# Gate/up weights: four of eight steps by seven products instead of three, two low parts by an accumulating transfer, and a pool mixer that takes its means first

## The chip, the cores and the metric

One core of one Trainium2 chip runs the whole program. The metric is the device time of one execution in microseconds; of several runs the median is given.

## The reference

A trunk of two layers on x of 256 tokens by 2048 channels, all in fp32. Each layer adds a token mixer and then a SwiGLU feed-forward net, both behind an RMS norm; at the end stands one more norm.

```python
for i in range(DEPTH):                      # 2
    hn = rmsnorm(h, norm_mix[i])
    if i % 2 == 0: mix = pool_mixer(hn, pool_w, pool_scale)   # means over 2, 4, 8, 16 tokens
    else:          mix = diff_attention(hn, ...)              # 8 heads, ALiBi, w_qkv, w_o
    h = h + mix
    h = h + swiglu(rmsnorm(h, norm_ffn[i]), w_gate[i], w_up[i], w_down[i])
return rmsnorm(h, final_norm)

swiglu(h, wg, wu, wd) = (silu(h @ wg) * (h @ wu)) @ wd        # 2048 -> 5632 -> 2048
```

The pool mixer takes, in each of four groups of 512 channels, the trailing mean less the token itself, and multiplies it with that group's 512 x 512 matrix.

## The kernel before

**Products.** Every weight element is used for 256 tokens. TensorE multiplies in fp32r, so an operand is split in a high part (a cast) and a low part (the operand less its high part), and a product is hi x hi + hi x lo + lo x hi: three matmuls. `split` does that for activations, `halves` (L114, L115) for weights: ACT casts whi, DVE subtracts to make wlo.

**Steps.** Weights come as raw tiles of 1 MB, 128 x 4 x 512, which `load` (L108) fetches on SP's queue into three buffers. A tile holds four blocks B12, B11, B22, B21 of a 2 x 2 product of blocks: two slices of the inner dimension by two column halves (for gate/up: 512 gate columns and 512 up columns); the left side's blocks are two slices by two tiles of 128 tokens. A *plain* step makes all eight block products, 8 x 3 = 24 matmuls of 128 x 512. A step *by seven products* makes seven, 21 matmuls, by the scheme of Strassen and Winograd: it needs sums of the weight's blocks (`sums`, tsum, L120 to L123, on DVE), their high and low parts (`sum_halves`, thi on ACT at L129, tlo on DVE at L130), and the activation's sums S1 to S4, made once in `pair` (L244 to L249). whi and wlo have three buffers each; tsum, thi and tlo have one each, in the pool of the feed-forward net.

**Groups.** `group` (its matmuls are L172) runs eight steps into eight PSUM banks, which the code names by the products: M1, M6, M7, P5, P3, P4, M2 and X are b0 to b7. A plain step adds to C11, C12, C21, C22, which are the banks M2, P3, P4 and X, that is b6, b4, b5 and b7. `combined` (L176 to L193) then makes the four results: ACT copies M1 (L182) and P5 (L186), DVE adds (L183 to L192), and each bank is free when its reader is done. Gate/up has eleven groups per layer, in chunks of 4, 4 and 3; behind each group ACT takes silu of the gate (L354) and DVE multiplies (L355), and TensorE transposes the result (L231) for the down product. Behind each chunk follow two down groups. SEVEN = (1, 4, 6) names the gate/up steps by seven: 5 x 24 + 3 x 21 = 183 matmuls per group. SEVEN_DOWN, SEVEN_QKV and SEVEN_O do it for the others.

**Order.** The program is written step by step, but a scheduler sets the order of each engine's instructions when the kernel is built; on the chip each engine then runs its list in order. Which matmuls stand next to each other at a group's end, and where a cast stands among ACT's copies, is thus decided there.

**Start and end.** At the start the pool mixer multiplies first and takes its means after: x comes transposed (x_t) for the products and as rows (x_n) for the residual; when the squares of the rows are summed (L212), z = product x row factor x scale (L310), and two or three small matmuls with a band matrix (L313, L315) take the means. Group 0 is multiplied in plain fp32 (L290), the others split (L303). At the end, behind the last row factor, eight DVE operations (L386) make x x factor x final gain, and four transfers carry it out.

Of the kernel before, what the change touches and what calls it, by code (L numbers as in the profile page):

```python
# [16 lines left out]
P = 128  # L17
# [9 lines left out]
WARM = 10  # L27
WINDOWS = (2, 4, 8, 16)
# [7 lines left out]
SEVEN = (1, 4, 6)  # L36
SEVEN_DOWN = (1, 4)
SEVEN_QKV = (1, 4)
SEVEN_O = ()

# [8 lines left out]
def trunk_kernel(ctx, tc, x_t, x_n, gains, scale_in, final_in, subln, lam_in, band, dist,  # L49
# [61 lines left out]
    def halves(raw, lo_block=0):  # L111
        hi = whl.tile([P, 4, 512], F32R, name="whi")
        lo = whl.tile([P, 4, 512], F32R, name="wlo")
        nc.scalar.copy(hi[:, lo_block:], raw[:, lo_block:])  # L114
        nc.vector.tensor_tensor(lo[:, lo_block:], raw[:, lo_block:], f32(hi[:, lo_block:]), ALU.subtract)  # L115
        return hi, lo
# [20 lines left out]
    def group(steps, pool):  # L137
# [15 lines left out]
        for (a, seven, src), step in zip(steps, plan):  # L153
            raw = load(src)
            t = sums(pool, raw) if seven else None
            w = [halves(raw, B11 if seven else 0)]
            if seven:
                w.append(sum_halves(pool, t))
            for b, parts in step:
# [3 lines left out]
                for at, which, block in parts:  # L163
                    hi, lo = w[which]
                    if seven:
                        ah, al = a[:, 0, at], a[:, 1, at]
                    else:
                        k, t = at
                        ah, al = (a[:, k, i, t * P:(t + 1) * P] for i in range(2))
# [26 lines left out]
    def rsqrt(ss, n, cols):  # L196


        v, s, t, r = (tmp.tile([P, 8], F32, name=f"rs_{x}") for x in "vstr")
# [9 lines left out]
    def square_sum(ss, t, j):  # L209

        sq = tmp.tile([P, 512], F32, name="sq", bufs=1)
        nc.scalar.activation(sq, x_tok[:, t, j * 512:(j + 1) * 512], AF.Square, accum_out=ss[:, t, j:j + 1])  # L212

    def row_scale(ss):
        tot = tmp.tile([P, 2], F32, name="ss_tot")
        nc.vector.tensor_reduce(tot, ss, AX.X, ALU.add)
        r = tmp.tile([P, 2], F32, name="r_tok", bufs=3)
# [40 lines left out]
    xp = operand()  # L258
    xq = operand(SEVEN)
    ss = tmp.tile([P, 2, 4], F32, name="ss")  # L260
    with tc.tile_pool(name="start", bufs=1, reuse_waits="tile") as st:
        band_sb = st.tile([P, 4, 3, P], F32, name="band_sb")
        scale_sb = st.tile([P, D], F32, name="scale_sb")
        xf = st.tile([P, NK, S], F32, name="xf")
        nc.scalar.dma_start(out=gain_sb, in_=gains)

        warm = tmp.tile([P, 8], F32, name="warm", bufs=1)
# [5 lines left out]
        def load_x(k0, k1):  # L273
            nc.sync.dma_start(out=xf[:, k0:k1, :], in_=x_t[:, k0 * S:k1 * S].rearrange("p (k s) -> p k s", s=S))


        w0 = st.tile([P, 4, 512], F32, name="w0")
        load_x(0, 1)
        nc.sync.dma_start(out=w0[:, 0:2], in_=pool_w[0][:, 0:2])
        load_x(1, 4)  # L280
        nc.sync.dma_start(out=w0[:, 2:4], in_=pool_w[0][:, 2:4])
        load_x(4, 8)
        x0 = st.tile([P, 4, S], F32, name="x0")
        zp = [None] * 4

        zp[0] = [acc() for _ in range(2)]
        for k in range(4):
            nc.vector.tensor_scalar(x0[:, k, :], xf[:, k], gain_sb[:, 0, k:k + 1], None, ALU.mult)
            for t in range(2):
                nc.tensor.matmul(zp[0][t], x0[:, k, t * P:(t + 1) * P], w0[:, k], start=(k == 0), stop=(k == 3))  # L290

        def group_product(g):
            zp[g] = [acc() for _ in range(2)]
            hi, lo = halves(load(pool_w[g]))
            if g < 3:
                load_x(4 * g + 4, 4 * g + 8)
            for k in range(4 * g, 4 * g + 4):
                a = tile_of(xp, k)
                split(a, xf[:, k], gain_sb[:, 0, k:k + 1])
                for t in range(2):  # L300
                    ah, al = (a[:, i, t * P:(t + 1) * P] for i in range(2))
                    for i, (u, w) in enumerate(((ah, hi), (ah, lo), (al, hi))):
                        nc.tensor.matmul(zp[g][t], u, w[:, k % 4], start=(k % 4 == 0 and i == 0),  # L303
                                         stop=(k % 4 == 3 and i == 2))

        def group_mean(g):
            cols = slice(g * 512, (g + 1) * 512)
            z = st.tile([P, 2, 512], F32, name="z", bufs=2)
            for t in range(2):
                nc.vector.scalar_tensor_tensor(z[:, t], zp[g][t], r[:, t:t + 1], scale_sb[:, cols], ALU.mult, ALU.mult)  # L310
            for t in range(2):
                ps = aux()
                nc.tensor.matmul(ps, band_sb[:, g, t], z[:, t], start=True, stop=(t == 0))  # L313
                if t:
                    nc.tensor.matmul(ps, band_sb[:, g, 2], z[:, 0], start=False, stop=True)  # L315
                nc.vector.tensor_tensor(x_tok[:, t, cols], ps, x_tok[:, t, cols], ALU.add)
                square_sum(ss, t, g)
            transposed(xq, g, 2, SEVEN)

        group_product(1)  # L320
        nc.sync.dma_start(out=x_tok, in_=x_n)
        ss_in = tmp.tile([P, 2, 4], F32, name="ss")
        for t in range(2):
            for j in range(4):
                square_sum(ss_in, t, j)
        r = row_scale(ss_in)
        nc.sync.dma_start(out=band_sb, in_=band)
        nc.sync.dma_start(out=scale_sb, in_=scale_in)
        nc.sync.dma_start(out=dist_sb, in_=dist)
        group_product(2)  # L330
        group_mean(0)
        group_product(3)
        group_mean(1)
        group_mean(2)
# [261 lines left out]
```

## Time and profile before

| | |
|---|---|
| three runs | 1902.51, 1901.35, 1902.2 us; median 1902.2 |
| the profiled execution | 1902.04 us by itself, its span 1900.1 us |
| mean granted TensorE clock | 0.989 |
| instructions | 20741 |
| HBM read, written | 355.39 MB, 2.10 MB |
| DMA | 189 GB/s over the span, 52% of 16 engines |

The profile is one execution on the chip. Times are microseconds from the start of the span; PE is TensorE, DVE VectorE, ACT ScalarE, POOL GpSimd and SP SyncE; L172 is line 172 of the kernel. A line of the timeline gives start, duration, engine, operation with output and inputs, and in brackets the idle time ahead of it with what ended it. The duration of a matmul is that of its way through the array; how often one starts is read from the distance of starts. A row of the chain of waits is a piece of the path that ended last.

### The profile page before, as it was taken

What the parts mean: (1) busy time and instruction counts of PE and PEld (TensorE: products, weight loads), DVE (VectorE), ACT (ScalarE), POOL (GpSimd) and SP (SyncE); (2) the same over time, 40 slices, a digit from 0 to 9 for tenths busy, and PEclk for the clock granted to TensorE, in tenths of its full rate; (3) what the DMA queues carried; (4) which work ended last, traced back from release to release, by engine and by line L of the source; (5) the groups of instructions that cost most, each with busy time, mean ns of one, the idle gap of its engine ahead of it and who ended that gap; (6) DMA issues with size and microseconds to landing.
All of it is one profiled execution on the core that took longest, in us unless ns stands there. A gap on an engine that the chain in (4) does not pass through costs nothing.

```text
span 1900.1 us, 20741 instructions
## 1 busy us (share of the span) xinstructions
PE 1852.9 (98%) x8204; PEld 1506.3 (79%) x8204; DVE 1571.1 (83%) x1591; ACT 1013.6 (53%) x983; POOL 0.7 (0%) x6
## 2 busy tenths in 40 slices
PE   8999999999999999999999999999999999999997
PEld 5678888888888887777777778888888888888885
DVE  5888987888878998987786645998878999878887
ACT  5555544555544556655555544655544555445554
POOL 0000000000000000000000000000000000000000
PEclk8999999999999999999999999999999999999998
DMA  8355555555555554544444444555555555565552
GB/s 308 141 191 199 200 191 201 187 205 207 196 189 211 185 199 176 187 168 155 166 147 153 177 140 170 199 198 181 206 212 201 198 200 199 194 225 186 201 200 101
DMA packets 51152, 358.82 MB, mean 189 GB/s; under 512 B 6000, under 2 KB 6256, under 8 KB 8432
## 3 DMA queue, kind: packets, MB, share of 16 engines
q1 hardware_dynamic: 50080, 355.36, 52.0%
q10 hardware_dynamic: 976, 2.15, 0.3%
q8 instruction: 64, 1.05, 0.2%
q14 instruction: 32, 0.26, 0.0%
HBM read 355.39 MB, written 2.10 MB: 188 GB/s over the span
## 4 chain that ended last, share of the span: by engine, by line
PE 92%; DVE 4%; ACT 2%; issue 1%; DMA 1%; SPq 0%; DVEq 0%; ACTq 0%
PE b L172 88%; PE b L231 2%; DVE wlo L115 1%; DMA x_tok<-x_n 1%; PE b L303 1%; ACT sq L212 1%; ACT whi L114 1%; PE b L313 0%; PE b L438 0%; DVE tsum L120 0%; DVE y L386 0%; DVE x_tok L373 0%; DVE s_sb L440 0%; DVE oT L224 0%; DVE xp L224 0%
## 5 line engine op out<-in xcount | busy, mean ns | idle before, releaser
L172 PE MATMUL b<-whi,xp 128*128 128x512 f32 x2804 | 905.8, 393 | 8.8 <-DVE c L189 3.0
L114 ACT CAST whi<-raw 128x2048 fp32r<-128x2048 f32 (+1 forms) x331 | 587.2, 1780 | 601.9 <-PE b L172 465.5
L115 DVE TENSOR_TENSOR wlo<-raw,whi 128x2048 fp32r<-128x2048 f32 (+1 forms) x331 | 701.0, 2123 | 219.2 <-ACT whi L114 217.7
L172 PEld LDWEIGHTS b<-whi,xp 128*128 128x128 f32 x2804 | 526.9, 189 | 126.9 <-ACT e L244 5.7
L172 PE MATMUL b<-wlo,xp 128*128 128x512 f32 x1402 | 549.9, 392 | 0.6 <-DVE wlo L115 0.5
L172 PE MATMUL b<-whi,h 128*128 128x512 f32 x1168 | 370.3, 390 | 1.1 <-ACT e L244 1.1
L172 PEld LDWEIGHTS b<-wlo,xp 128*128 128x128 f32 x1402 | 264.7, 189 | 55.6 <-DVE wlo L115 1.4
L172 PEld LDWEIGHTS b<-whi,h 128*128 128x128 f32 x1168 | 218.7, 188 | 47.0 <-ACT e L244 2.1
L130 DVE TENSOR_TENSOR tlo<-tsum,thi 128x2048 fp32r<-128x2048 f32 x102 | 233.1, 2286 | 19.8 <-ACT thi L129 19.3
L172 PE MATMUL b<-wlo,h 128*128 128x512 f32 x584 | 227.5, 390 | 0.1
L172 PE MATMUL b<-thi,xp 128*128 128x512 f32 x624 | 220.0, 394 | 0.0
L129 ACT CAST thi<-tsum 128x2048 fp32r<-128x2048 f32 x102 | 194.8, 1910 | 30.7 <-DVE tsum L123 30.7
L172 PEld LDWEIGHTS b<-thi,xp 128*128 128x128 f32 x624 | 116.5, 188 | 24.0 <-ACT thi L129 0.8
L120 DVE TENSOR_TENSOR tsum<-raw 128x1024 f32<-128x1024 f32 x102 | 124.5, 1220 | 7.6 <-DMA raw<-w_down 4.8
L172 PEld LDWEIGHTS b<-wlo,h 128*128 128x128 f32 x584 | 109.6, 188 | 23.5 <-DVE wlo L115 0.6
L172 PE MATMUL b<-tlo,xp 128*128 128x512 f32 x312 | 121.8, 390 | 0.0
L172 PE MATMUL b<-whi,oT 128*128 128x512 f32 x256 | 82.7, 402 | 2.2 <-DVE oT L224 2.2
L122 DVE TENSOR_TENSOR tsum<-tsum,raw 128x512 f32<-128x512 f32 x102 | 70.4, 690 | 2.4
L123 DVE TENSOR_TENSOR tsum<-tsum,raw 128x512 f32<-128x512 f32 x102 | 70.1, 687 | 1.9
L172 PEld LDWEIGHTS b<-tlo,xp 128*128 128x128 f32 x312 | 58.6, 188 | 12.1 <-DVE tlo L130 0.2
L172 PE MATMUL b<-thi,h 128*128 128x512 f32 x192 | 67.6, 393 | 0.3 <-ACT thi L129 0.3
L172 PEld LDWEIGHTS b<-whi,oT 128*128 128x128 f32 x256 | 49.2, 193 | 12.9 <-issue 2.6
(121 smaller groups left out, 1137.0 us busy)
## 6 DMA issues: line engine op xcount, KB each, us to landing
raw<-w_gu SPq DMA_DIRECT2D x176, 1024.0 KB, 4.8
raw<-w_down SPq DMA_DIRECT2D x88, 1024.0 KB, 4.8
raw<-w_qk SPq DMA_DIRECT2D x32, 1024.0 KB, 4.9
raw<-w_v SPq DMA_DIRECT2D x16, 1024.0 KB, 4.8
raw<-w_o SPq DMA_DIRECT2D x16, 1024.0 KB, 4.8
raw<-pool_w SPq DMA_DIRECT2D x3, 1024.0 KB, 16.9
x_tok<-x_n SPq DMA_DIRECT2D x1, 2048.0 KB, 13.7
xf<-x_t SPq DMA_DIRECT2D x3, 512.0 KB, 10.0
```

Source lines behind the costliest of these rows:

```text
L114: nc.scalar.copy(hi[:, lo_block:], raw[:, lo_block:])
L115: nc.vector.tensor_tensor(lo[:, lo_block:], raw[:, lo_block:], f32(hi[:, lo_block:]), ALU.subtract)
L120: nc.vector.tensor_tensor(t[:, T1:T3 + 1], raw[:, B11:B22 + 1], raw[:, B12:B12 + 1].broadcast_to([P, 2, 512]), ALU.add)
L122: nc.vector.tensor_tensor(t[:, T2], t[:, T1], raw[:, B22], ALU.add)
L123: nc.vector.tensor_tensor(t[:, T4], t[:, T2], raw[:, B21], ALU.add)
L129: nc.scalar.copy(hi, t)
L130: nc.vector.tensor_tensor(lo, t, f32(hi), ALU.subtract)
L172: nc.tensor.matmul(ps[b], x, y[:, block], start=first, stop=(left[b] == 0))
L212: nc.scalar.activation(sq, x_tok[:, t, j * 512:(j + 1) * 512], AF.Square, accum_out=ss[:, t, j:j + 1])
L231: nc.tensor.transpose(ps[:, i, 1 - t if seven else t], src(i, t), ident)
L303: nc.tensor.matmul(zp[g][t], u, w[:, k % 4], start=(k % 4 == 0 and i == 0), stop=(k % 4 == 3 and i == 2))
```

## The change

**Steps.** SEVEN becomes (1, 3, 5, 7): four of the eight gate/up steps go by seven, 4 x 24 + 4 x 21 = 180 matmuls, and the last step is now one of them. In the first group of each layer only step 7 does (7 x 24 + 21 = 189). SEVEN_QKV becomes (1, 5).

**Low parts.** In steps 0 and 4 of gate/up (ADDED) the low part is not subtracted by DVE. ACT writes -w, rounded to fp32r, into a tile with a tag of its own ("added", one buffer) and casts whi as before; then a transfer issued by GpSimd adds w, fetched once more from HBM, onto -w in place. That is 2 x 22 = 44 transfers of 1 MB.

**Start.** x_t is gone. x_n comes first in four pieces, the squares and the row factor follow, and the band matrix is scaled by the row factor; each group then takes its means by matmuls (x as rows times band) and multiplies them with the weights, two groups in plain fp32 and two split.

**End.** x x final gain is made beside the last down group; behind the row factor only a scaling is left, four on ACT and four on DVE. Some small buffers are shared to make room.

```diff
-SEVEN = (1, 4, 6)
+SEVEN = (1, 3, 5, 7)
-SEVEN_QKV = (1, 4)
+SEVEN_QKV = (1, 5)
+ADDED = (0, 4)
...
-    def halves(raw, lo_block=0):
+    def halves(raw, lo_block=0, added=None):
         hi = whl.tile([P, 4, 512], F32R, name="whi")
+        if added:
+            pool, src = added
+            lo = pool.tile([P, 4, 512], F32R, name="wlo", tag="added")
+            nc.scalar.activation(lo, raw, AF.Copy, scale=-1.0)
+            nc.scalar.copy(hi, raw)
+            nc.gpsimd.dma_start(out=lo, in_=src, accum_op=ALU.add)
+            return hi, lo
...
-            w = [halves(raw, B11 if seven else 0)]
+            w = [halves(raw, B11 if seven else 0, (pool, src) if i_step in added else None)]
...
+        for t in range(2):
+            for i in range(2):
+                cols = slice(i * 1024, (i + 1) * 1024)
+                nc.sync.dma_start(out=x_tok[:, t, cols], in_=x_n[:, t, cols])
...
+            r = rsqrt(tot[:, 0:1], D, 1)
+            part = band_sb[:, :, 0:2] if t == 0 else band_sb[:, :, 2:3]
+            nc.vector.tensor_scalar(part, part, r, None, ALU.mult)
...
-                    cs = combined(group([(xq[p], p in SEVEN, w_gu[layer][g, p]) for p in range(NP)], hp), hp)
+                    by_seven = SEVEN[-1:] if g == 0 else SEVEN
+                    cs = combined(group([(xq[p], p in by_seven, w_gu[layer][g, p]) for p in range(NP)], hp, ADDED), hp)
...
-                        nc.vector.scalar_tensor_tensor(y[:, t], x_tok[:, t, cols], r[:, t:t + 1],
-                                                       final_sb[j // 2][:, cols.start % 1024:cols.start % 1024 + 512],
-                                                       ALU.mult, ALU.mult)
+                        if t:
+                            nc.vector.tensor_scalar(ys[j][:, t], ys[j][:, t], r[:, t:t + 1], None, ALU.mult)
+                        else:
+                            nc.scalar.activation(ys[j][:, t], ys[j][:, t], AF.Copy, scale=r[:, t:t + 1])
```

The new file is longer: L172 (the matmuls) becomes L189, L114 (whi) L127 and L123 for the added steps, where L122 writes -w; L115 (wlo) becomes L128 and the transfer is L124; L120, L122, L123 (tsum) become L133, L135, L136; L129 and L130 (thi, tlo) L142 and L143; the copies of `combined` L199 and L203, its DVE operations L200 to L209; the transposes L248; silu and the product behind it L379 and L380; the work at the end L408, L419, L421.

What the scheduler makes of it is shown at two boundaries of layer 0. A name's number is a running one: a tile with a higher number is of a later step or group. First TensorE at the boundary of gate/up groups 6 and 7, before: b7_3147 and b4_3133 belong to step 0 of group 7 (weights 3122, 3123), and thi_3164, tlo_3165 and whi_3160 to its step 1.

```order
L172 MATMUL b7_3147<-wlo_3123,xp_91 128x512
L231 MATMUL b5_3099<-ident_75,c12_3081 128x128
L231 MATMUL b6_3113<-ident_75,c12_3081 128x128
L172 MATMUL b7_3147<-whi_3122,xp_91 128x512 x2
L172 MATMUL b7_3147<-wlo_3123,xp_91 128x512
L172 MATMUL b7_3147<-whi_3122,xp_91 128x512
L172 MATMUL b1_3175<-thi_3164,xp_92 128x512
L172 MATMUL b2_3179<-thi_3164,xp_92 128x512
L172 MATMUL b3_3183<-thi_3164,xp_92 128x512
L172 MATMUL b4_3133<-whi_3160,xp_92 128x512
L172 MATMUL b4_3133<-wlo_3161,xp_92 128x512
L172 MATMUL b1_3175<-tlo_3165,xp_92 128x512
```

The same place after; thi_3099 and tlo_3100 are those of step 7 of group 6, whi_3205, wlo_3206, thi_3209 and tlo_3210 those of step 1 of group 7.

```order
L189 MATMUL b4_2868<-whi_3095,xp_90 128x512
L189 MATMUL b5_2875<-thi_3099,xp_90 128x512
L189 MATMUL b5_2875<-tlo_3100,xp_90 128x512
L189 MATMUL b5_2875<-thi_3099,xp_90 128x512
L189 MATMUL b0_3213<-whi_3205,xp_84 128x512
L189 MATMUL b0_3213<-wlo_3206,xp_84 128x512
L189 MATMUL b0_3213<-whi_3205,xp_84 128x512
L189 MATMUL b1_3220<-thi_3209,xp_84 128x512
L189 MATMUL b2_3224<-thi_3209,xp_84 128x512
L189 MATMUL b3_3228<-thi_3209,xp_84 128x512
L189 MATMUL b1_3220<-tlo_3210,xp_84 128x512
L189 MATMUL b1_3220<-thi_3209,xp_84 128x512
```

Before, the last step's thi lay 39 matmuls ahead of the first use of the next (thi_3025 belongs to step 6), and 44 ahead of the first use of tlo. Now 3 matmuls lie between the last use of thi_3099 and the first of thi_3209, and 6 before the first of tlo_3210; step 0's matmuls follow behind. At the other boundaries of two gate/up groups the new order has 14 and 21 (1 to 2, 4 to 5), 15 and 31 (5 to 6), 30 and 31 (0 to 1, 2 to 3), and 3 and 6 again (8 to 9, 9 to 10); into the down groups it has 3 and 24 behind group 3, 13 and 38 behind group 7, and 13 and 50 behind group 10. Layer 1 has the same.

ScalarE at this place before: c11_3080 and c22_3083 are the copies of M1 and P5, whi_3195 is the cast of step 2 of the next group.

```order
L129 CAST thi_3025<-tsum_3017 128x2048
L114 CAST whi_3122<-raw_3120 128x2048
L182 COPY c11_3080<-b0_2865 128x512
L186 COPY c22_3083<-b3_2880 128x512
L114 CAST whi_3160<-raw_3154 128x1536
L129 CAST thi_3164<-tsum_3156 128x2048
L354 ACTIVATE c11_3080<-c11_3080,r_tok_450 128x512
L114 CAST whi_3195<-raw_3193 128x2048
L354 ACTIVATE c21_3082<-c21_3082,r_tok_450 128x512
```

And after, where whi_3240 is the cast of step 2; it takes the buffer of step 7's whi, whose last reader is the first row of TensorE's rows above (P3, bank b4).

```order
L142 CAST thi_3099<-tsum_3091 128x2048
L127 CAST whi_3205<-raw_3199 128x1536
L199 COPY c11_3124<-b0_2903 128x512
L203 COPY c22_3127<-b3_2918 128x512
L127 CAST whi_3240<-raw_3238 128x2048
L379 ACTIVATE c11_3124<-c11_3124,r_tok_460 128x512
L142 CAST thi_3209<-tsum_3201 128x2048
L379 ACTIVATE c21_3126<-c21_3126,r_tok_460 128x512
```

Before, thi of the next group (thi_3164) stood ahead of the first silu and of the cast of step 2. Now the cast of step 2 and the first silu stand ahead of thi_3209.

VectorE at the boundary of groups 5 and 6, before; c12, c21, c11 and c22 are the results that `combined` makes of group 5's banks.

```order
L115 TENSOR_TENSOR wlo_2820<-raw_2817,whi_2819 128x2048
L183 TENSOR_TENSOR c12_2784<-b1_2575,c11_2783 128x512
L123 TENSOR_TENSOR tsum_2853<-tsum_2853,raw_2851 128x512
L185 TENSOR_TENSOR c21_2785<-b2_2579,c12_2784 128x512
L184 TENSOR_TENSOR c11_2783<-b6_2526,c11_2783 128x512
L187 TENSOR_TENSOR c12_2784<-c22_2786,c12_2784 128x512
L115 TENSOR_TENSOR wlo_2858<-raw_2851,whi_2857 128x1536
L188 TENSOR_TENSOR c22_2786<-c22_2786,c21_2785 128x512
L189 TENSOR_TENSOR c12_2784<-b4_2533,c12_2784 128x512
```

And after:

```order
L128 TENSOR_TENSOR wlo_2896<-raw_2889,whi_2895 128x1536
L200 TENSOR_TENSOR c12_2821<-b1_2606,c11_2820 128x512
L133 TENSOR_TENSOR tsum_2891<-raw_2889 128x1024
L201 TENSOR_TENSOR c11_2820<-b6_2557,c11_2820 128x512
L202 TENSOR_TENSOR c21_2822<-b2_2610,c12_2821 128x512
L135 TENSOR_TENSOR tsum_2891<-tsum_2891,raw_2889 128x512
L204 TENSOR_TENSOR c12_2821<-c22_2823,c12_2821 128x512
L136 TENSOR_TENSOR tsum_2891<-tsum_2891,raw_2889 128x512
L205 TENSOR_TENSOR c22_2823<-c22_2823,c21_2822 128x512
L206 TENSOR_TENSOR c12_2821<-b4_2564,c12_2821 128x512
```

Bank b4, which the next group's step 0 takes, is freed by L189 before and by L206 after. Before, one low part and a sum of the next group stood among the operations ahead of it; now it is the whole tsum, in three operations, behind the low part of step 1. TensorE takes up b4 at this boundary right behind the three matmuls of M1 of step 1; the same holds at the boundaries 2 to 3 and 0 to 1.

More of the change, by code (lines that the diff above doesn't have):

```diff
@@ L135, in trunk_kernel, with group @@
     C11, C12, C21, C22 = M2, P3, P4, X
-    def group(steps, pool):
+    def group(steps, pool, added=()):
         plan = []
@@ L284, in trunk_kernel @@
-        zp = [None] * 4
[L286 to L290, printed above, removed]
+        band_sb = st.tile([P, 4, 3, P], F32, name="band_sb")
+        for t in range(2):
+            for i in range(2):
+                cols = slice(i * 1024, (i + 1) * 1024)
+                nc.sync.dma_start(out=x_tok[:, t, cols], in_=x_n[:, t, cols])
@@ L292, in group_product @@
+        scale_sb = st.tile([P, D], F32, name="scale_sb")
+        nc.scalar.dma_start(out=scale_sb, in_=scale_in)
+        nc.scalar.dma_start(out=dist_sb, in_=dist)
+        zp = [None] * 4
         def group_product(g):
             zp[g] = [acc() for _ in range(2)]
[L294 to L304, printed above, removed]
@@ L307, in group_mean, with residual @@
+        def residual(g):
             cols = slice(g * 512, (g + 1) * 512)
-            z = st.tile([P, 2, 512], F32, name="z", bufs=2)
             for t in range(2):
[L310 to L316, printed above, removed]
+                y = st.tile([P, 512], F32, name="y", bufs=2)
+                nc.vector.tensor_tensor(y, zp[g][t], scale_sb[:, cols], ALU.mult)
+                nc.vector.tensor_tensor(x_tok[:, t, cols], y, x_tok[:, t, cols], ALU.add)
@@ L317, in group_mean @@
                 square_sum(ss, t, g)
             transposed(xq, g, 2, SEVEN)
+        group_product(0)
         group_product(1)
[L321 to L329, printed above, removed]
+        residual(0)
```

106 lines of the change are left out of this document (70 added, 36 removed).

## The prediction

> **What bounds the kernel now.** I read the page first: the table of engines and the chain of work that ended last.
>
> ```profile
> PE 1852.9 (98%) x8204; PEld 1506.3 (79%) x8204; DVE 1571.1 (83%) x1591; ACT 1013.6 (53%) x983; POOL 0.7 (0%) x6
> PE 92%; DVE 4%; ACT 2%; issue 1%; DMA 1%; SPq 0%; DVEq 0%; ACTq 0%
> ```
>
> TensorE is the bound: 98% busy, 92% of the chain. So I asked next where it waits. In the two stretches that hold ten of eleven gate/up groups and the down groups of each layer (107 to 703 and 1231 to 1883 us) it never does: in the table of stretches, whose columns are length, busy time of PE, PEld, DVE, ACT and POOL, granted clock, DMA share and GB/s, busy time equals length. The third row is one gate/up group.
>
> ```profile
> 107.00:703.00 596.00, 596.00 (x2660) 491.91 (x2659) 519.28 (x448) 311.13 (x230) 0.00 (x0) 1.00 0.55 198
> 1231.00:1883.00 652.00, 652.00 (x2913) 537.99 (x2912) 569.04 (x493) 340.29 (x260) 0.00 (x0) 1.00 0.54 194
> 197.60:240.00 42.40, 42.40 (x192) 34.81 (x191) 38.81 (x36) 23.60 (x20) 0.00 (x0) 1.00 0.55 199
> ```
>
> A group takes 42.4 us; DVE works 38.8 of it, ACT 23.6. DVE is the second bound, with 3.6 us to spare, but sets nothing today. The price of one product is the distance of two matmul starts in the timeline:
>
> ```profile
> 86.27 0.39 PE L172 MATMUL b<-thi,xp 128*128 128x512 f32 x1
> 86.50 0.39 PE L172 MATMUL b<-tlo,xp 128*128 128x512 f32 x1
> ```
>
> that is 0.23; over many rows 0.2277 us (183 of them and the transposes make the 42.4).
>
> **Fewer products.** Twenty groups go from 183 to 180 matmuls, the two first groups from 183 to 189: 20 x 3 - 2 x 6 = 48 fewer, 48 x 0.2277 = **-10.9 us**. That is the whole gain on the bounding engine in the layers, and it comes only if TensorE goes on without waiting.
>
> **What changes at a group's end.** This is the step I rest on. The trace of before has one place, in the first group, where a released buffer is followed by the same casts; here are PE, ACT and DVE there (start, duration, engine):
>
> ```profile
> 90.58 0.62 PE L172 MATMUL b<-whi,xp 128*128 128x512 f32 x2
> 94.83 1.20 PE L172 MATMUL b<-thi,xp 128*128 128x512 f32 x4
> 97.69 0.40 PE L172 MATMUL b<-tlo,xp 128*128 128x512 f32 x1
> 105.15 0.79 PE L172 MATMUL b<-whi,xp 128*128 128x512 f32 x1 [2.98 <-DVE c L189]
> ```
>
> ```profile
> 91.05 1.91 ACT L114 CAST whi<-raw 128x2048 fp32r<-128x2048 f32 x1 [4.59 <-PE b L172]
> 92.87 1.91 ACT L129 CAST thi<-tsum 128x2048 fp32r<-128x2048 f32 x1
> 104.79 0.72 ACT L354 ACTIVATE c<-c,r_tok 128x512 f32<-128x512 f32 x1
> ```
>
> ```profile
> 93.00 2.29 DVE L115 TENSOR_TENSOR wlo<-raw,whi 128x2048 fp32r<-128x2048 f32 x1 [2.00 <-ACT whi L114]
> 95.21 2.29 DVE L130 TENSOR_TENSOR tlo<-tsum,thi 128x2048 fp32r<-128x2048 f32 x1
> 97.41 1.75 DVE L115 TENSOR_TENSOR wlo<-raw,whi 128x1536 fp32r<-128x1536 f32 x1
> 99.08 0.68 DVE L183 TENSOR_TENSOR c<-b,c 128x512 f32<-128x512 f32 x1
> 99.68 1.22 DVE L120 TENSOR_TENSOR tsum<-raw 128x1024 f32<-128x1024 f32 x1
> 100.81 0.68 DVE L184 TENSOR_TENSOR c<-b,c 128x512 f32<-128x512 f32 x1
> ```
>
> TensorE's last use of a buffer (start 90.58) released ACT 0.47 later; whi and thi in a row put the first matmul of thi at 94.83, 4.25 after that start, and wlo and tlo put the first of tlo at 97.69, 7.11 after. From start to start on a full queue a cast costs 1.82, a low part 2.21 (1536 columns: 1.67), a combining operation 0.60, the first sum 1.13.
>
> At a boundary of the old order the last step is plain: thi was last used 39 to 42 matmuls (9 us) before the next thi is wanted, and the products M1, M6, M7 and P5 end 24 matmuls (5.5 us) before the group does, so all but the last sums are done under them. In the new order the last step is by seven, and both covers go. thi, tlo and tsum have one buffer each, so thi of the next group's step 1 is cast after the last matmul of this group. Five kinds of boundary follow from the order; t = 0 is the start of the last matmul of P3, and after three more matmuls the group is over.
>
> *Kind A* (groups 6 to 7, 8 to 9, 9 to 10 of a layer; the rows are in the section on the change). PE wants thi 7 matmuls on, at 1.59. ACT: whi of step 2 waits for P3, 0.47 to 2.29; silu, with 0.6 (its row has 0.72 by itself), to 2.9; thi to 4.8; PE goes on at 4.87, **3.28 late**. DVE: wlo of step 2 from 2.4 to 4.64, a combining operation to 5.24, tlo to 7.53; PE has 3 thi matmuls to do first and would want tlo at 5.55; it gets it at 7.72, **2.17 late**. Sum 5.45 us.
>
> *Kind B* (2 to 3, 5 to 6, and 0 to 1). PE wants bank b4 at 1.59 for step 0. It is freed by L206, ahead of which stand eight DVE operations, begun at about -0.4, when wlo of step 1 is done: 7 x 0.60 + 1.13, and 0.60 of its own, put its end at 5.5; stall 4.1, then 1.2 for the two last results: 5.3 (5.65 for 0 to 1, where the activation table is loaded too). *Kind C* (1 to 2, 4 to 5): three short waits, 0.56 + 0.47 + 0.99 = 2.0. *Kind D*: the chain into the first down group after group 3, 3.8. *Kind E*: into the others, 1.0 each.
>
> Per layer 3 x 5.45 + 2 x 5.3 + 5.65 + 2 x 2.0 + 3.8 + 2 x 1.0 = 42.4; two layers: **+85 us**. Below it lies 0, if the order ran as it does now; half of it, 42, if only the first wait of each place remained. I take the whole, because both chains are the quoted ones, and the waits cannot move: the order on each engine is fixed.
>
> **The clock after a stall.** The stall of 2.98 us before 105.15 was followed by a stretch at half the clock:
>
> ```profile
> 102.17:105.15 2.98, 0.01 (x1) 0.00 (x0) 2.98 (x6) 2.95 (x3) 0.00 (x0) 0.99 0.07 22
> 105.15:108.40 3.25, 3.25 (x8) 2.57 (x9) 2.87 (x4) 2.78 (x3) 0.00 (x0) 0.50 0.87 302
> ```
>
> 8 matmuls in 3.25 us where 14.3 would fit: 1.4 us lost. The new order has 14 stalls of 3.28 or more, so 0 to 20; part of it falls into waits that come anyway. I take a third, **+7**.
>
> **The accumulating transfers.** 44 low parts leave DVE. It loses 2 x 2.21 us per group and gains one step by seven (about 6.4 - 2.2), so stays near 38; ACT gains 44 casts of 1.8. The nearest rows for the transfer itself are the plain load of the same 1 MB and the one of 2 MB beside other loads:
>
> ```profile
> raw<-w_gu SPq DMA_DIRECT2D x176, 1024.0 KB, 4.8
> x_tok<-x_n SPq DMA_DIRECT2D x1, 2048.0 KB, 13.7
> ```
>
> It reads two streams, is issued by POOL and shares the engines with SP's loads, so I take 8 us, between 4.8 and 13.7. What it may take without a wait is set by its one buffer ("added"): the matmuls from the last use of one to the first of the next, less the cast of -w. For step 0 that is 12.4 to 16.5 us: no wait. For step 4 it is 35 x 0.2277 - 1.9 = 6.0 in group 2, 7.0 in 5 and 7, 6.9 in 9, 9.5 in 10, 13 elsewhere. At 8: 2.0 + 1.0 + 1.0 + 1.1 = 5.1 per layer, **+10**; at 4.8 nothing; at 12 about +47. Layer 1's first group has 2.8 us of lead: **+5**.
>
> The Trainium skill, DMA: Bandwidth & Descriptors, "Anatomy of one DMA", fits a GpSimd transfer by 2.0 us plus its bytes over 436,000 per us: an estimate of 4.4 us for this one, by which the two terms would be 0 and the sum 15 lower. No trace here shows such a transfer.
>
> **Start.** First the chain, then the timeline, then L172 alone in the stretch:
>
> ```profile
> 3.76 1.08 SPq L274
> 4.89 13.74 DMA x_tok<-x_n
> 23.94 0.73 ACT sq L212 x2
> 26.39 0.76 DVE z L310
> 64.82 26.17 PE b L172 x114
> ```
>
> ```profile
> 6.18 7.11 PE L290 MATMUL b<-w,x 128*128 128x512 f32 x16 [0.49 <-DMA w<-pool_w]
> ```
>
> ```profile
> 6.18:64.82 58.64, 7.44 (x25) 4.21 (x25) 0.91 0.63 249
> ```
>
> At 64.82 the first group had 25 of its matmuls done, so the start proper ends at 64.82 - 5.7 = 59.1. In the new kernel TensorE begins when x_tok is there (3.8 + 2 x 4.8 = 13.4), its last half row squared (1.5) and the factor known (26.39 less 24.67, 1.7): about 17. Then it has 16 plain products of 0.87 (7.11 for 8), 16 means of 384 columns (0.65), 48 split products and 32 transposes of about 0.12: 39 us. It ends at 56: -3. The first group then lacks the 2.98 us stall and its slow stretch: -4.4. But its first accumulated part is wanted as soon as it is begun: 8 us and the hand-over, +9. Together **+2**; with x_tok at its old 13.7 us, +6; with a short transfer, -7.
>
> **Tail.** From the timeline of before:
>
> ```profile
> 1891.03 5.39 DVE L386 SCALAR_TENSOR_TENSOR y<-x_tok,r_tok,final_sb 128x512 f32<-128x512 f32 x8
> 1892.47 3.04 SPq L389 DMA_DIRECT2D out_t<-y  x2
> ```
>
> Eight operations of 0.67 on DVE become four on DVE and four on ACT: up to -2.7; the 2 MB that leave set part of the end, so **-1.3**. The products with the final gain lie ahead, beside the last down group.
>
> **Sum.** 1902.0 (the profiled run's own time; its span is 1900.1, the median of the runs 1902.2) - 10.9 + 85 + 7 + 10 + 5 + 2 - 1.3 = **1998.8 us**.
>
> **The rivals.** *The covers hold (8%).* TensorE goes on at the group ends and the transfers come in time: 1902.0 - 10.9 - 1.3 - 7 (start) = 1883. For it speaks that no boundary of before has a wait; against it that the plain last step under which those casts ran is gone.
>
> *Half of the waits (20%).* The second wait of a place may be shorter, since the stall at the first lets DVE catch up: 42 for 85, and 3 for the clock: 1902 - 10.9 + 42 + 3 + 10 + 5 + 2 - 1 = 1952. Against it: in kind A the tlo chain begins at the same matmul as the thi chain, so waiting for thi does not shorten it.
>
> *The transfer is the bound (14%).* At 12 us instead of 8 its two terms grow from 15 to 47 + 13 and the start by 4, so 2048; from about 7 us on it costs anything, from 12 on it leads. For it: two more MB per group on a queue that has carried no such thing before; against: DMA has 45% of its time free.
>
> *It does nothing but trade (2%).* If stalls of half a microsecond at each boundary eat the 10.9, the time stays within 0.2%, which is about what a measurement of this kernel can tell from no change (its three runs lie 0.06% apart).
>
> The forecast itself, all covers gone and an 8 us transfer, has 56%, with its own range from 1965 to 2030 (clock 0 to 20, transfer terms 0 to 30). The range for all reaches down to 1925, below the half case with a short transfer (1937), and up to 2050; it leaves out the first rival, the last and half of the third, some 17%. Faster 0.08, same 0.02, slower 0.90.
>
> **What would show it.** In the waits of TensorE after: L189 waiting for ACT thi L142 and DVE tlo L143, some 3.3 and 2.2 us each, six times; for DVE c L206 about 4, six times; for DMA wlo only one or two us at step 4, and 8 once at the start. A group of 44 to 48 us instead of 42.4. The granted clock below 1.00 in slices all through. If TensorE is busy 100% between 107 and 700 again, the step on the group's end is wrong; if its longest waits are for wlo of L124, it is the transfer that was mis-sized.

## The result and the profile after

The changed kernel takes 2068.0 us (median of four runs, 2067.62 to 2073.21), the kernel before 1901.8 beside it: a ratio of 1.088 with a 95% interval of 1.0866 to 1.0893. The forecast, 1998.8 with a range of 1925 to 2050, had the sign and missed the size by 69 us. The profiled execution is the longest of the four, 2073.21 us; its span is 2071.4, its mean granted clock 0.958 (before 0.989).

The page of the kernel after, engines and chain:

```profile
PE 1903.2 (92%) x8188; PEld 1527.1 (74%) x8188; DVE 1550.0 (75%) x1617; ACT 1121.4 (54%) x1047; POOL 39.2 (2%) x50
PE 70%; DVE 13%; DMA 7%; ACT 6%; issue 3%; ACTq 0%; SPq 0%; DVEq 0%
```

TensorE still bounds the kernel, but is no longer fed: 16 instructions fewer and yet 50 us more busy, and 168.2 us idle (2071.4 - 1903.2) where it had been 47.2. DVE has 21 us less to do and idles more. What TensorE waits for (total us, times, longest):

```profile
PE b L189 <- DMA wlo<-w_gu: 42.5, 11, 9.7
PE b L189 <- ACT thi L142: 29.0, 14, 3.3
PE b L189 <- DVE c L206: 25.6, 8, 4.2
PE b L189 <- DVE tlo L143: 15.7, 13, 2.0
```

Those are the waits that the prediction named: thi, tlo and L206 come to 70.3 us. One boundary of kind A (groups 6 to 7 of layer 0), on TensorE, ScalarE and VectorE; the first row is the last matmul of P3, t = 0 of the working:

```profile
490.49 0.39 PE L189 MATMUL b<-whi,xp 128*128 128x512 f32 x1
...
495.29 0.96 PE L189 MATMUL b<-thi,xp 128*128 128x512 f32 x3 [3.05 <-ACT thi L142]
498.01 0.80 PE L189 MATMUL b<-tlo,xp 128*128 128x512 f32 x1 [1.76 <-DVE tlo L143]
```

```profile
490.91 1.91 ACT L127 CAST whi<-raw 128x2048 fp32r<-128x2048 f32 x1
492.73 0.71 ACT L379 ACTIVATE c<-c,r_tok 128x512 f32<-128x512 f32 x1
493.35 1.88 ACT L142 CAST thi<-tsum 128x2048 fp32r<-128x2048 f32 x1
```

```profile
492.86 2.29 DVE L128 TENSOR_TENSOR wlo<-raw,whi 128x2048 fp32r<-128x2048 f32 x1
495.07 0.68 DVE L204 TENSOR_TENSOR c<-c,c 128x512 f32<-128x512 f32 x1
495.67 2.29 DVE L143 TENSOR_TENSOR tlo<-tsum,thi 128x2048 fp32r<-128x2048 f32 x1
```

Read from 490.49, TensorE takes up thi at 4.80 and tlo at 7.52, where the working had 4.87 and 7.72. Between the last copy and thi ACT is never idle, nor is DVE up to tlo; the chain is just that long. Now the granted clock (the column behind the busy times) at this place:

```profile
488.00:491.85 3.85, 3.85 (x19) 3.19 (x17) 3.81 (x6) 2.32 (x4) 0.00 (x0) 1.00 0.80 330
492.24:495.29 3.05, 0.00 (x1) 0.00 (x1) 3.05 (x4) 3.00 (x3) 0.00 (x0) 1.00 0.79 269
495.29:501.90 6.61, 4.85 (x12) 3.60 (x13) 6.61 (x9) 0.72 (x1) 0.00 (x0) 0.56 0.55 195
```

The stall is over at 495.29, and for 6.6 us more the clock is near one half: 12 matmuls, where 19 had run in 3.85 us. The last thing to see is an accumulating transfer, in the chain around 190 us (step 4 of group 2):

```profile
186.20 1.93 ACT wlo L122
...
188.47 8.70 DMA wlo<-w_gu
...
197.22 2.80 PE b L189 x11
```

ACT writes -w, the transfer is issued 0.34 us later and takes 8.70, and TensorE goes on 0.05 behind its landing.

### The profile page after: what moved, and what is told of

Same layout as the page of the kernel before. It is cut to its first block, busy times and chain, and to the rows that moved or that the text cites. A ratio compares the mean times of both kernels' runs of the same rounds, so it can differ in the third digit from the quotient of the medians.

```text
span 2071.4 us, 20870 instructions
## 1 busy us (share of the span) xinstructions
PE 1903.2 (92%) x8188; PEld 1527.1 (74%) x8188; DVE 1550.0 (75%) x1617; ACT 1121.4 (54%) x1047; POOL 39.2 (2%) x50
## 3 DMA queue, kind: packets, MB, share of 16 engines
q1 hardware_dynamic: 49216, 351.30, 45.9%
q0 software_dynamic: 6336, 46.14, 12.0%
## 4 chain that ended last, share of the span: by engine, by line
PE 70%; DVE 13%; DMA 7%; ACT 6%; issue 3%; ACTq 0%; SPq 0%; DVEq 0%
PE b L189 66%; DMA wlo<-w_gu 5%; DVE wlo L128 4%; DVE tlo L143 3%; ACT whi L127 2%; PE b L248 2%; ACT thi L142 1%; DVE tsum L133 1%; ACT wlo L122 1%; DMA raw<-w_gu 1%; DMA raw<-pool_w 1%; DVE c L204 1%; DVE c L201 1%; PE b L332 1%; DVE c L200 0%
## 5 line engine op out<-in xcount | busy, mean ns | idle before, releaser
L189 PE MATMUL b<-whi,xp 128*128 128x512 f32 x2644 | 882.6, 402 | 30.1 <-DVE c L206 23.8
L128 DVE TENSOR_TENSOR wlo<-raw,whi 128x2048 fp32r<-128x2048 f32 (+1 forms) x286 | 590.7, 2068 | 293.7 <-ACT whi L127 292.7
L127 ACT CAST whi<-raw 128x2048 fp32r<-128x2048 f32 (+1 forms) x286 | 494.6, 1733 | 496.3 <-PE b L189 430.7
L189 PEld LDWEIGHTS b<-whi,xp 128*128 128x128 f32 x2644 | 510.5, 194 | 147.9 <-DVE c L206 26.5
L189 PE MATMUL b<-wlo,xp 128*128 128x512 f32 x1322 | 533.0, 403 | 45.7 <-DMA wlo<-w_gu 42.5
L189 PE MATMUL b<-whi,h 128*128 128x512 f32 x1168 | 374.7, 394 | 2.4 <-DVE c L206 1.8
L143 DVE TENSOR_TENSOR tlo<-tsum,thi 128x2048 fp32r<-128x2048 f32 x118 | 269.9, 2287 | 90.2 <-ACT thi L142 89.7
L189 PEld LDWEIGHTS b<-wlo,xp 128*128 128x128 f32 x1322 | 256.6, 194 | 106.2 <-DMA wlo<-w_gu 47.3
L189 PE MATMUL b<-thi,xp 128*128 128x512 f32 x752 | 269.1, 399 | 18.6 <-ACT thi L142 18.6
L189 PEld LDWEIGHTS b<-whi,h 128*128 128x128 f32 x1168 | 219.9, 189 | 51.6 <-DVE c L206 3.1
L142 ACT CAST thi<-tsum 128x2048 fp32r<-128x2048 f32 x118 | 224.6, 1904 | 30.2 <-DVE tsum L136 28.6
L189 PE MATMUL b<-wlo,h 128*128 128x512 f32 x584 | 228.8, 392 | 1.3 <-DVE wlo L128 1.3
L189 PEld LDWEIGHTS b<-thi,xp 128*128 128x128 f32 x752 | 143.4, 192 | 50.8 <-ACT thi L142 22.2
L189 PE MATMUL b<-tlo,xp 128*128 128x512 f32 x376 | 153.2, 407 | 15.4 <-DVE tlo L143 15.4
L133 DVE TENSOR_TENSOR tsum<-raw 128x1024 f32<-128x1024 f32 x118 | 144.1, 1221 | 6.8 <-DMA raw<-w_gu 4.2
L122 ACT ACTIVATE wlo<-raw 128x2048 fp32r<-128x2048 f32 x44 | 84.4, 1918 | 105.2 <-PE b L189 98.1
L189 PEld LDWEIGHTS b<-wlo,h 128*128 128x128 f32 x584 | 110.5, 189 | 24.1 <-DVE wlo L128 1.7
L123 ACT CAST whi<-raw 128x2048 fp32r<-128x2048 f32 x44 | 84.0, 1908 | 35.1 <-PE b L189 34.6
L189 PEld LDWEIGHTS b<-tlo,xp 128*128 128x128 f32 x376 | 72.9, 194 | 36.2 <-DVE tlo L143 21.3
L189 PE MATMUL b<-whi,oT 128*128 128x512 f32 x256 | 82.6, 401 | 2.2 <-DVE oT L241 2.2
L135 DVE TENSOR_TENSOR tsum<-tsum,raw 128x512 f32<-128x512 f32 x118 | 81.2, 688 | 2.4
L136 DVE TENSOR_TENSOR tsum<-tsum,raw 128x512 f32<-128x512 f32 x118 | 81.1, 687 | 2.2
## 6 DMA issues: line engine op xcount, KB each, us to landing
w<-pool_w SPq DMA_DIRECT2D x2, 1024.0 KB, 11.8
```

Source lines behind the costliest of these rows:

```text
L122: nc.scalar.activation(lo, raw, AF.Copy, scale=-1.0)
L123: nc.scalar.copy(hi, raw)
L133: nc.vector.tensor_tensor(t[:, T1:T3 + 1], raw[:, B11:B22 + 1], raw[:, B12:B12 + 1].broadcast_to([P, 2, 512]), ALU.add)
L135: nc.vector.tensor_tensor(t[:, T2], t[:, T1], raw[:, B22], ALU.add)
L136: nc.vector.tensor_tensor(t[:, T4], t[:, T2], raw[:, B21], ALU.add)
L142: nc.scalar.copy(hi, t)
```

## The experiments

Two sums are read from each profile: *idle*, the span less TensorE's busy time, and *lost clock*, the span times one less the mean granted clock. They overlap in part, since the clock is also low in some idle time; the mean clock has three digits, so lost clock is good to about 1 us. The medians are of all runs, the two sums of the one profiled execution.

| kernel | steps by seven | transfers in steps | median us | ratio to before (95%) | idle | lost clock |
|---|---|---|---|---|---|---|
| before | 1 4 6 | none | 1901.8 | | 47.2 | 20.9 |
| after | 1 3 5 7 | 0 4 | 2068.0 | 1.0866 to 1.0893 | 168.2 | 87.0 |
| e1 | 1 4 6 | none | 1899.7 | 0.9987 to 1.0006 | 48.0 | 19.0 |
| e2 | 0 2 4 6 | 1 5 | 1931.7 | 1.0153 to 1.0183 | 73.3 | 27.0 |
| e3 | 1 3 5 7 | none | 1998.5 | 1.0505 to 1.0536 | 113.9 | 59.9 |
| e4 | 1 3 5 7, filled | 0 4 | 2042.7 | 1.0743 to 1.0796 | 129.0 | 55.4 |
| e5 | 1 4 6 | 0 5 | 1993.5 | 1.0470 to 1.0511 | 114.7 | 55.9 |
| e6 | 1 3 5 7 | 0 | 2035.4 | 1.0692 to 1.0724 | 141.4 | 77.3 |
| e7 | 1 3 5 7, filled | none | 1982.6 | 1.0410 to 1.0445 | 85.9 | 25.8 |
| e8 | 0 2 4 6 | 1 5, not in first groups | 1907.1 | 1.0020 to 1.0046 | 52.5 | 22.9 |
| e9 | 0 2 4 6 | none | 1945.0 | 1.0216 to 1.0244 | 74.3 | 17.5 |
| e10 | 1 3 5 7, two thi in layer 0 | none | 1994.9 | 1.0473 to 1.0512 | 111.6 | 51.7 |
| e11 | 1 4 6, w_qk as before | none | 1899.4 | 0.9979 to 0.9997 | 46.4 | 13.3 |
| e12 | 0 2 4 6, first groups too | 1 5, not in first groups | 1955.5 | 1.0273 to 1.0303 | 86.0 | 25.3 |

The theory: the last step by seven makes TensorE wait at the group ends, the transfers make it wait where their lead is short, and each stall costs again in clock. The rivals were that the new start costs, that four steps by seven are too many wherever they stand, that DVE is short, and that the slow clock lies under waits and is free.

### e1: the new start and end alone

```diff
-SEVEN = (1, 3, 5, 7)
+SEVEN = (1, 4, 6)
-ADDED = (0, 4)
+ADDED = ()
-                    by_seven = SEVEN[-1:] if g == 0 else SEVEN
+                    by_seven = SEVEN
```

> The new start and the new end with the old steps: by seven in 1, 4 and 6 in every group, no accumulating transfers. Theory (the group ends and the transfers make the whole loss): 1902 with the start and the tail a few us shorter or longer, 1893 to 1905, and no wait of TensorE over 1 us in the gate/up groups behind the first. Rival (the new start costs by itself: TensorE waits 6.6 us for the scaled band, then for the means): 1908 to 1918.

1899.7: no difference. TensorE's longest wait:

```profile
PE b L322 <- DVE band_sb L305: 6.3, 1, 6.3
```

It waits once for the scaled band, and then the start has caught up; no gate/up boundary has a wait of 1 us. So the loss is all in the steps and the transfers, and the gain that the prediction gave the start and the tail (8.7 us without the transfer's wait) is not there as a whole.

### e2: the last step plain

```diff
-SEVEN = (1, 3, 5, 7)
+SEVEN = (0, 2, 4, 6)
-SEVEN_QKV = (1, 5)
+SEVEN_QKV = (0, 4)
-ADDED = (0, 4)
+ADDED = (1, 5)
```

> Four steps by seven as in the changed kernel, but steps 0, 2, 4, 6, so that the last step is plain again; the transfers in steps 1 and 5 (leads of 12.9 us and more by the order; w_qk by seven in 0 and 4). Theory: the waits at group ends (70 us of thi, tlo and L206) and those for the transfers at the second added step (24 us) go, and their slow clock; left are the 10.9 us of fewer products and two first waits for a transfer of some 5 us: 1890 to 1905. Rival (four steps by seven are too much for single buffers of thi, tlo and tsum wherever they stand, gaps of 21 to 30 matmuls): 1930 to 1980, with waits for thi and tlo inside the groups.

1931.7, 136 us under the changed kernel, with the same number of products and of transfers. (Both the steps by seven and the transfers have moved; e9 moves the steps alone.) The head of its waits:

```profile
PE b L189 <- DMA wlo<-w_gu: 16.2, 2, 10.0
```

The 42.5 us for transfers are down to the two first ones, and thi, tlo and L206 to 4.0, 5.0 and 1.4. It lies above the range of the theory and at the edge of the rival's. Of the 43 us over 1888.8 the two first waits and 8.0 us more of lost clock than in e1 make 24, and 9 more are small waits (73.3 - 48.0 - 16.2), as the rival had said of the short gaps; the other 10 are in no list. Where the steps and the transfers lie is most of the loss, but not all.

### e3: the changed kernel without transfers

```diff
-ADDED = (0, 4)
+ADDED = ()
```

> The changed kernel with all low parts made by DVE, no accumulating transfers. Theory: the 42 us of waits for them go, and some 15 to 20 of slow clock; the waits at group ends stay at about 70: 2000 to 2020. Rival (DVE, 4.4 us more per group, about 43 in a group of 41 for TensorE, becomes the bound and gives it back): 2035 to 2070, with DVE over 80% busy and waits for wlo.

1998.5, just below the theory's range: the transfers cost 69.5 us in all, against 24 in the sum. The group ends alone, without transfers, stand 98.8 above e1, or 109.7 above what 48 products fewer would leave of it:

```profile
PE b L189 <- ACT thi L142: 43.3, 22, 4.2
PE b L189 <- DVE c L206: 23.7, 13, 5.1
```

67 us for those two; idle is up by 66 (113.9 - 48.0) and lost clock by 41 (59.9 - 19.0), 107 together. DVE, 82% busy, did not take the place of the transfers.

### e4 and e7: matmuls that fill the stall

14 matmuls that are overwritten by the next product into their bank, at six boundaries per layer.

```diff
+                    if fill and seven and first and b == M1:
+                        for _ in range(fill):
+                            nc.tensor.matmul(ps[b], ah, hi[:, block], start=True, stop=True)
                     for x, y in ((ah, hi), (ah, lo), (al, hi)):
...
-                    cs = combined(group([...], hp, ADDED), hp)
+                    cs = combined(group([...], hp, ADDED, 14 if g in (1, 3, 6, 7, 9, 10) else 0), hp)
```

In e4 all else is the changed kernel:

> The changed kernel with 14 matmuls more, overwritten by the next product into the same bank, at six boundaries per layer (into groups 1, 3, 6, 7, 9 and 10), where TensorE stands 3 to 4 us idle: they take 3.2 us each and 38 us in all. Theory (the stalls cost a second time, since the clock is halved behind them): the waits for thi and L206 there shrink to under 1 us, the granted clock stays at 1.00 behind them, and the time falls by 10 to 30, to 2038 to 2058, although work was added. Rival (the slow stretches lie under later waits and cost nothing): no change, 2065 to 2072. Rival (the added matmuls delay what follows): 2075 to 2106.

In e7 it is e3:

> The kernel of the third experiment (no transfers, 1998.5) with the 14 overwritten matmuls at the same six boundaries per layer. Theory (the clock costs again behind a stall): half-clock time falls from 92 us to 40 to 60, the time by 15 to 30: 1968 to 1984. Rival (the gain with transfers came from their waits): 1995 to 2005, or up to 2036 if the matmuls only add.

2042.7 and 1982.6, both in the theory's ranges: 25.3 and 15.9 us *less* with 38.3 us of work *more* (2 x 6 x 14 x 0.2277). The profiled execution of e4 is the longest of its four (2053.6), 19.6 us under that of the changed kernel. At the boundary shown above e4 has

```profile
490.55 3.34 PE L189 MATMUL b<-whi,xp 128*128 128x512 f32 x14
...
494.47 0.98 PE L192 MATMUL b<-thi,xp 128*128 128x512 f32 x3
```

with no wait for thi behind the fill. The expected clock of 1.00 is not reached there: tlo still comes 1.73 us late, and over the 6.6 us from 494.47 the granted clock is 0.76, where it was 0.56. Over the whole kernel the waits are

```profile
PE b L192 <- DVE tlo L143: 16.0, 13, 1.7
PE b L192 <- ACT thi L142: 10.4, 8, 3.1
PE b L192 <- DVE c L209: 5.9, 8, 1.0
```

where they were 15.7, 29.0 and 25.6 (L209 is L206 of the changed kernel). The idle time falls by 39.2, as much as was added, so that alone would change nothing; lost clock falls from 87.0 to 55.4. In e7 the idle time falls by 28.0, less than was added, and lost clock from 59.9 to 25.8. That the stalls are paid twice is shown: all that the fill gains is the clock.

### e5: transfers with the old steps

```diff
 (e1, and)
-ADDED = ()
+ADDED = (0, 5)
```

> As the kernel of the first experiment (new start and end, steps 1, 4 and 6 by seven, 1899.7), with accumulating transfers in steps 0 and 5 (plain steps; leads by the order 8.8 to 9.0 us at step 5 and 14 or more at step 0, none in the first groups). Theory (a transfer costs where its lead is shorter than the 8.6 to 9.7 us measured, and nowhere else): two first waits of 6 to 10, 0 to 0.8 us at each of 22 steps 5, 3 to 6 of slow clock: 1917 to 1940, and no wait at step 0 behind the first groups. Rival (the 1 MB more per transfer slows the loads and the casts behind them everywhere): 1945 to 1975.

1993.5, 93.7 above e1, beyond both ranges. TensorE's wait, and two pieces of the chain:

```profile
PE b L189 <- DMA wlo<-w_gu: 61.4, 29, 11.6
```

```profile
195.42 9.26 DMA wlo<-w_gu
...
222.74 12.85 DMA wlo<-w_gu
```

The rows are the transfers of steps 0 and 5 of one group. The expectation had the two leads the wrong way round: in the order of the matmuls 47 to 49 stand between the last use of step 5's tile and the first of the next step 0's, 71 and more between step 0's and step 5's, so inside a chunk the lead of 8.8 to 9.0 is step 0's. TensorE wants the tile there 8.3 to 8.6 us after the issue, the transfer takes 9.0 to 10.1, and all 16 of these are late, by 0.4 to 1.9 and 14.6 in sum.

But the larger part, 27.6, comes from 11 of the steps 5, where the order leaves 14 us. There the cast of -w began 3.9 to 6.7 us after its buffer's last use, so that 9.2 to 11.0 were left from the issue, and the transfer took 11.4 to 13.4, beside four or five loads of SP.

So the 27 waits behind the two first ones come to 42 us, and idle and lost clock rise by 66.7 and 36.9, together a little over the 93.7. The theory's mechanism, a lead too short, holds as long as the lead is counted from the issue. The rival's sign is there too: ACT and DVE waited 81 us for loads of w_gu, 2 in e1; but in e8 ACT waits 87 us for them without harm, so what they cost here is not separated. The loss needs no step by seven at a group's end.

### e6: the transfer of step 4 taken away

```diff
-ADDED = (0, 4)
+ADDED = (0,)
```

> The changed kernel with the accumulating transfer in step 0 only; DVE makes the low part of step 4. Theory: 24 us of waits at step 4 go, and 10 to 20 of slow clock with them; the first groups still wait 9.7 and 8.7: 2020 to 2036. Rival (DVE's work comes back as other waits): 2040 to 2068.

2035.4, the upper end of the theory's range: 32.6 us less for 24.2 us of waits. The waits at the group ends stay, those for transfers shrink to the first of each layer:

```profile
PE b L189 <- ACT thi L142: 29.0, 14, 3.2
PE b L189 <- DVE c L206: 27.6, 8, 4.4
PE b L189 <- DMA wlo<-w_gu: 18.3, 2, 9.7
```

### e8, e9, e12: the steps 0, 2, 4 and 6, with and without transfers

e8 is e2 with `ADDED if g else ()`, e9 is e2 with `ADDED = ()`, e12 is e8 with `by_seven = SEVEN` in the first groups too.

> The kernel of the second experiment (steps 0, 2, 4, 6 by seven, transfers in 1 and 5, 1931.7), with DVE making all low parts in the first group of each layer. Theory: its two waits for a transfer (16.2 us) go, and 2 to 4 us of slow clock: 1911 to 1916, still over before by the small waits for tlo and thi (gaps of 21 to 28 matmuls). Rival (the first wait only moves to the next group's transfer): 1922 to 1932.

> Steps 0, 2, 4, 6 by seven and all low parts by DVE, no transfers: it differs from the third experiment (1998.5) only in where the steps by seven lie. Theory (the last step by seven is what costs, not their number): 1888.8 (1899.7 less 48 products) and 5 to 20 us of small waits: 1894 to 1909. Rival (with 4.4 us more per group DVE becomes the bound once TensorE no longer waits): 1915 to 1945, with waits for wlo and tlo and DVE over 86%.

> The kernel of the eighth experiment (1907.1) with four steps by seven in the first group of each layer too, where DVE makes all low parts: 18 products fewer, 4.1 us. Theory (TensorE follows wherever the last step is plain and no transfer is late): 1902 to 1905. Rival (DVE, which makes all low parts and four tsum and tlo there, makes TensorE wait): 1907 to 1914.

e8: 1907.1, 24.6 under e2 where 16.2 of waits went, better than the theory's range, and the best of the kernels with four steps by seven. It still is 0.33% over before (interval 0.20 to 0.46%). No transfer is on the list of waits any more, with leads of 12.9 us and more by the order. From the issue the shortest is 9.7, and such a transfer lands just in time:

```profile
PE b L189 <- ACT thi L142: 4.1, 3, 2.0
...
PE b L189 <- DVE tlo L143: 3.1, 6, 0.7
```

e9: 1945.0, the rival's end, though DVE is 84% busy, not over 86%, and the waits are for thi and L206 more than for low parts. Without the transfers DVE and ACT are late all along, a little at a time. TensorE is busy 14.3 us longer than in e1 (1850.7), with 48 products fewer and no more lost clock, since a start that is late by less than a matmul's way through the array counts as busy:

```profile
PE 1865.0 (96%) x8188; PEld 1493.3 (77%) x8188; DVE 1637.0 (84%) x1661; ACT 1045.6 (54%) x1003; POOL 0.7 (0%) x6
```

```profile
PE b L189 <- ACT thi L142: 11.4, 17, 0.9
PE b L189 <- DVE c L206: 7.6, 4, 3.0
...
PE b L189 <- DVE tlo L143: 5.3, 7, 1.0
```

Against e8 that is the worth of the transfers where they come in time: 38 us. And against e3 it is the price of the last step by seven without any transfer: 53.5 (the steps of w_qk moved too, but the attention part, 414.3 us for 416.3, differs little).

e12: 1955.5, beyond both ranges. In the order that the scheduler makes of it four leads in the first chunk of each layer are 10.4 to 11.8 us; the cast of -w begins up to 4.4 us after its buffer's last use, and those transfers and the first of the layer are late, by 1.2 to 3.3:

```profile
PE b L189 <- DMA wlo<-w_gu: 21.1, 10, 3.3
PE b L189 <- ACT thi L142: 15.1, 10, 3.8
```

Neither the theory nor the rival had looked at the leads of that order. With 12.9 and more (e8) none was late, with 10.4 to 11.8 all were. The 48 us over e8 lie in the first chunk of each layer; behind it the groups are as long as in e8 (40.8, 41.8 and 42.4 us). That the late transfers are their whole cause is not shown: DVE, which the rival named, has more to do there as well.

### e10: two buffers of thi in layer 0

```diff
-        hi = pool.tile([P, 4, 512], F32R, name="thi")
+        hi = pool.tile([P, 4, 512], F32R, name="thi", bufs=2 if in_ffn else 1)     # in_ffn: layer 0
```

> The kernel of the third experiment (1998.5) with two buffers of thi instead of one in the first layer alone; the second layer is its own control (755.9 us for layer 1 there, 763.1 for layer 0). Theory (the single buffer of thi makes TensorE wait for thi at a group's end): the waits for thi of layer 0, some 21 us, go, and layer 0 is 20 to 30 us shorter: 1968 to 1980. Rival (the banks that are freed at the end and the order of the casts make it, thi only shows it): layer 0 changes by under 5 us, 1993 to 2003.

The rival holds. By the matmul starts layer 0 takes 760.5 us (763.1 in e3), and layer 1, the control, 752.1 (755.9). The waits:

```profile
PE b L190 <- ACT thi L143: 39.2, 20, 4.1
PE b L190 <- DVE c L207: 22.0, 13, 5.0
```

So it is not thi's one buffer. In ACT's list the cast of step 2, which waits for P3, and the first silu still stand ahead of thi at this boundary; a free buffer behind them helps nothing. No run changes that order by itself, so what another one would give stays open.

### e11: w_qk by seven in steps 1 and 4

```diff
 (e1, and)
-SEVEN_QKV = (1, 5)
+SEVEN_QKV = (1, 4)
```

> The kernel of the first experiment (new start and end, old steps, 1899.7) with w_qk by seven in steps 1 and 4 as before, not 1 and 5. Theory (the new start gains 7 us by the first layer's end, and the later step of w_qk gives 3 of it back): 1894 to 1898. Rival (the place in w_qk is worth nothing): 1898 to 1901.

1899.4, the rival: the place is worth nothing that can be told from e1. It is the only kernel whose interval lies below before, by 0.03 to 0.21%, so it is the one to keep, for what that is worth.

## Why the prediction was right in sign and wrong in size

- **Fewer products, -10.9.** Counted right (8188 matmul rows against 8236 in e1); nothing of it is seen in the time, since TensorE waits.
- **Group ends, +85.** Right in place and chain, a little high in size. Kind A was forecast at 3.28 and 2.17 late and came at 3.05 and 1.76 at four of the six places; L206 at 4.1 and came at 3.9 to 4.2. By the list thi, tlo and L206 make 70.3, and the small ones for wlo 4.5 more. The rival "half of the waits" is out: the tlo wait did follow the thi wait. One reason given for it was wrong: not the single buffer of thi holds the cast back (e10), but, by the order and the rows above, what stands ahead of it on ACT.
- **The clock after a stall, +7, 0 to 20.** This is the step that failed. It priced 14 stalls of 3.28 us or more at 1.4 us each and let two thirds of that fall into waits that come anyway. In the trace after, from 80 us to the end of the last layer, 25 stalls (from the end of one matmul to the start of the next) are longer than 2.0 us and 23 stretches run at half the clock, each begun in one of these stalls or some 2 us behind its end at most. And 13 of the 23 last 6.8 us or more, which is 3.4 us lost, not 1.4. Nor does most of it lie under waits: of the lost clock 59.9 us fall in TensorE's busy time, 14.2 before, so the term is 46 us for 7. e4 and e7 agree: without twelve stalls the time is 25 and 16 us shorter, although TensorE has more to do.
- **The transfers, +10, +5 and +9.** Right in mechanism, too small in size: 24 was forecast, 42.5 of waits came, and taking the transfers out gives 69.5 (e3), since their stalls cost clock too. 8 us were taken for one; from issue to landing the median is 8.8 (8.2 to 13.9), and 0.3 to 0.4 us lie between the cast and the issue. At step 4 TensorE waited 2.7, 1.7, 3.2 and 3.0 in layer 0, where 2.0, 1.0, 1.0 and 1.1 was the forecast, and in layer 1's first group 8.7 and 2.2 instead of 5. Step 0's leads of 12.4 and more were enough behind the first groups, as forecast. Two figures of the working do not come out, and neither moves the forecast: at a lead of 2.8 a transfer of 4.4 us still costs 1.6, not 0, and one of 12 us costs 9.2, not 13.
- **Start and tail, -8.7 without the transfer's wait.** e1 shows 0. The matmuls of the start and of layer 0 end 6.8 us earlier than before (54.4 + 706.2 against 46.4 + 721.0 from the first matmul), which is most of the 7.4; the attention part takes 3.4 and layer 1 1.1 longer, and from the last matmul to the end it takes about a microsecond more, not 1.3 less.

By terms: to 1998.8 the transfers' waits add 18, the clock 39 (46 for 7), start and tail 8, and the group ends take off 10: 2054, with 2073.2 for the profiled execution. Of the 19 that are left, some 10 are starts at full clock that come late by less than a matmul's way through the array and so count as busy (25.7 us over L189 in sum, 16.1 in e1); the prediction had no term for them. The rest stays open.

## What to carry to other kernels

A gain in products on the bounding engine is worth what the work around it lets through: before a step is made cheaper, look at what lay under the dear one, here the drain of eight banks and the casts of the next group. Count a stall on TensorE of 2 us and more about one and a half times, since the clock behind it is halved: here 46 us of clock came with 121 us more of idle time, and in e3 35 with 66. A transfer that takes work off an engine needs its whole time, in its slowest company, as lead, counted from its issue and not from the free buffer: in time (e8) these transfers were worth 38 us, late (e5) they cost 94.

## What the runs showed of the hardware

**An accumulating transfer took the DMA engines twice as long per byte as a plain load.** From the page after, the queues (packets, MB, share of 16 engines over the span) and the issues (count, KB, us to landing):

```profile
q1 hardware_dynamic: 49216, 351.30, 45.9%
q0 software_dynamic: 6336, 46.14, 12.0%
...
raw<-w_gu SPq DMA_DIRECT2D x176, 1024.0 KB, 6.4
...
wlo<-w_gu POOLq DMA_DIRECT2D x44, 1024.0 KB, 8.8
```

Per MB SP's queue takes 0.459 x 2071.4 / 351.30 = 2.7 us of all engines, POOL's 0.120 x 2071.4 / 46.14 = 5.4. The 115 loads of w_gu that overlap such a transfer land after a median of 7.8 us, the other 61 after 4.8. Each transfer ran beside two loads or more, so no run shows what one takes alone. The Trainium skill, DMA: Bandwidth & Descriptors, "Anatomy of one DMA", fits GpSimd's transfers by a formula that gives an estimate of 4.4 us for this size, half of the 8.8 measured; the measurement decides.

**A stall of 2 to 3 us was enough to lose the clock.** The stall of 3.05 us shown above was followed by 6.6 us near half clock. In the trace after, a half-clock stretch came with 23 of the 25 stalls of 2.1 us or more, among them three of the four of 2.1 to 2.3 us; of the eight between 1.0 and 1.5 none had a half-clock stretch of its own. In e4, where the fill leaves the stall for tlo by itself, three of six stalls of 1.7 us were followed by one. The Trainium skill, TensorE: Matmul & The Clock Gate, Part 1, puts the fall of the clock behind an idle window of about 3.4 us; the trace agrees with the length, since its half-clock stretches last 3.4 or 6.8 us (one 13.7), and not with the idle time that they need.
